# A two-block transformer in split precision: where weights' low parts are made, where modulation columns are computed, and when two groups of transposes are issued

## The chip, the cores and the metric

The kernel runs on one core of a Trainium2 chip. The metric is the time of one execution on the device in microseconds, lower is better; the median of several runs is given, and beside it the time of one execution that was taken with a profile. Engines are named as the profile names them: PE is TensorE (PEld its weight loads), DVE is VectorE, ACT is ScalarE, POOL is GpSimd, SP is SyncE, whose queue issues most DMAs.

## The reference, cut to what matters

The sequence has 512 tokens and the model 1024 channels, in fp32. The first block has two layers that are modulated by a condition vector `c`, and a second block follows.

```python
for layer in range(2):
    mod = silu(c) @ ada_w[layer] + ada_b[layer]
    sh_m, sc_m, g_m, sh_f, sc_f, g_f = split(mod, 6)
    h = modulate(rms_norm(x, pre_mix_g[layer]), sh_m, sc_m)
    y = gmlp_mixer(h, ...) if layer == 0 else fox_mixer(h, ..., k, v, dcum)
    x = x + g_m * rms_norm(y, post_mix_g[layer])
    h = modulate(rms_norm(x, pre_ffn_g[layer]), sh_f, sc_f)
    x = x + g_f * rms_norm(swiglu(h, ...), post_ffn_g[layer])
    if layer == 0:
        k, v, dcum = shared_kv(x, silu(c) @ kv_ada_w + kv_ada_b, ...)
...
def gmlp_mixer(h, ...):
    u, v = split(gelu(h @ w_in + b_in), 2)
    ...
    return y @ w_out
def shared_kv(x, mod_kv, ...):
    kvf = modulate(rms_norm(x), shift, scale) @ kv_w     # keys, values, forget gates
    k = rms_norm(k, k_norm_g)                            # per head of 64
    ...
```

The second block projects its normed input to an mLSTM's and a sparse attention's parts: `m_q`, `m_k`, `m_if` (gates) and `ix_q`, `ix_k`, `ix_w` (an indexer, whose scores choose 128 keys for each query) are among them. It ends with an output projection, a gated addition and a norm.

## The kernel before, in words

Every fp32 product is made of three TensorE products (`mm3`, L415 to L418): each operand is split into a high part, rounded to the type that TensorE takes, and a low part, the remainder. A weight tile of 128 x 1024 is loaded on SP's queue into one of four `raw` buffers (L271). ACT copies the high part (`whi`, L279). The low part (`wlo`, L282) is a subtraction on DVE, or, for every `share`-th tile, on POOL; a share of 0 keeps all on DVE. There are four buffers each for `whi` and `wlo`.

Products come in two forms. `gemm_a` takes one weight tile for one tile of 128 output features and 512 tokens: 24 matmuls, called a chunk. `gemm_b` (L459) holds four PSUM accumulators, one for each 128 tokens, for a group of 512 output features, and goes through the weight tiles of the group, two rows of 128 channels in each, again 24 matmuls a chunk. With `tail` the last chunks of the last group go token tile by token tile; with `head` the whole first group does, and its share is `hshare`. PSUM has two sets of four tiles: accumulators (`acc`) and transposes (`tp`).

The modulation is not a matmul. Its 96 columns are computed one by one on DVE: SP loads 128 x 1024 of `ada_w` into a `raw` buffer (L298), and one DVE operation multiplies by `silu(c)` and sums (L302, in place). `fill(n)` makes n such calls on average, each loading one column's weights and computing the column that was loaded by the call before, so 97 calls make 96 columns. `need(c0)` forces calls until a column is there. Calls are spread over the GEMMs by `nfill`: 1.25 for each chunk of `w_v` (L793), 0.75 for each of `w_ao` (L856), and 2 for each chunk of the gate-up of layer 0 from its 10th on (L432, L602). Ahead of `w_ao`, L854 needs the columns of the next norm. After a gate-up, L603 makes what calls are left.

The order of the stages around the change: the gMLP's `w_v` (groups 1 to 3, four chunks each), `w_u` (`gemm_a`), `w_ao` (two groups of eight chunks; its evacuation `post`, L550 to L573, starts with a DVE product at L558 and feeds `halves`, which transposes into the next GEMM's operands), the gate-up and the down product of the first feed-forward part, and then the shared keys and values. The keys (`w_k`, two groups, L1094) are normed for each head by `headnorm` (L873), and at the last token tile `kdone` (L1074) makes for each group 16 PE transposes (L959, in `pair_t`), four ACT copies (L1081), four DVE operations (L1082) and 16 DMA issues on POOL to a scratch (`spread`, L938). `forget` (L1098) follows, then the operands `hx` of the queries (eight times a load on SP, an ACT operation, and two DVE operations, L1123 to L1128), then the values (`w_vv`, two groups of four chunks, L1129, share 1, so all low parts on POOL) and the queries (`w_q`, L1133).

In the second block the indexer's projection `w_ix` ends with the gates. From them the kernel makes columns: four PE transposes at L1248 of ACT's `iwt` (L1244), eight at L1268, two DVE copies, and an ACT exponential; the DVE chain between ends at L1257 to L1259. Then comes `w_aqk` (L1291), whose evacuation `ev_a` runs after each chunk, and then the masks.

A scheduler at build time fixes the order in each engine's queue, from a model of durations and from what each instruction depends on, taking what comes first in the program among what is ready; a few stages, which the change does not touch, are written out by hand. Temporary tiles of 128 x 512 (`T`) rotate through nine buffers, which `kdone`, `forget` and the `hx` loop share.

Of the kernel before, what the change touches and what calls it, by code (L numbers as in the profile page):

```python
# [16 lines left out]
AF = mybir.ActivationFunctionType  # L17
# [3 lines left out]
P = 128  # L21
T_ = 512
NT = 4
# [21 lines left out]
KS = 2  # L45
KH = 3
VS = 1
# [144 lines left out]
def body(tc, nc, a):  # L192
    V, S_, G, PE = nc.vector, nc.scalar, nc.gpsimd, nc.tensor

    with ExitStack() as es:
# [31 lines left out]
        def acc():  # L227
            return tile_of(ps, "acc")
# [230 lines left out]
        def gemm_b(h, w, groups, kt, evac, head=False, tail=0, nfill=0, share=0, raws=(), hshare=1):  # L459
# [5 lines left out]
            for gi in groups:  # L465
# [8 lines left out]
                for c in range(nch - tm):  # L474
                    wh, wl = wsplit(w[gi, c], share=share, raw=raws.pop(0) if raws else None)
                    fill(nfill)
                    for t in range(NT):
                        part(t, c, wh, wl)
                ws = []
# [95 lines left out]
        def halves(h, g, sh, spill=None):  # L575

            xn = {}

            def done(t, n):
                xn[t] = n  # L580
                if t % 2:
                    to_T((t - 1, t), xn, g, sh, *h, spill=spill)
            return done
# [32 lines left out]
        with tc.tile_pool(name="l0", bufs=20) as p0:  # L616
# [176 lines left out]
            gemm_b(h, a["w_v"], range(1, 4), KD, ev_v, nfill=1.25, share=3, raws=early_w)  # L793
# [46 lines left out]
            def ev_u1(i, pt):  # L840
# [5 lines left out]
                else:  # L846
# [7 lines left out]
            gf, sf = gain(32, "pfg0"), need(24)  # L854
            hf = hpair()
            gemm_b((yh, yl), a["w_ao"], range(2), 16, post(gb, xs[0], xs[1], L, halves(hf, gf, sf)), tail=4,  # L856
                   nfill=0.75, share=2)
# [6 lines left out]
        def nxt0():  # L864
            hk.extend(hpair())
            return halves(hk, gain(104, "kvg"), need(96), xT)
# [5 lines left out]
        def headnorm(out, alloc, done=None):  # L872
# [3 lines left out]
            def evac(g, t, pt):  # L876
# [8 lines left out]
                if t == NT - 1:  # L885
                    rsq(ss[:, 32:64], ss[:, 0:32], 1.0 / 64)
                    for q in range(NT):
                        r = ss[:, 32 + q * 8:40 + q * 8]
                        V.tensor_mul(b3(raw[q], 8), b3(raw[q], 8), r.unsqueeze(2).broadcast_to((P, 8, 64)))
                        out[q, g] = raw[q]  # L890
                        if done:
                            done(g, q, raw[q])
# [172 lines left out]
        with tc.tile_pool(name="x", bufs=1) as px:  # L1065
# [8 lines left out]
            def kdone(g, t, ap):  # L1074

                if t < NT - 1:
                    return
# [17 lines left out]
            gemm_b(hk, a["w_k"], range(2), KD, headnorm(kt_, ka, kdone), head=True, share=KS, hshare=KH)  # L1095
# [3 lines left out]
            def forget():  # L1099
# [7 lines left out]
                pt = acc()  # L1107
# [21 lines left out]
            gemm_b(hk, a["w_vv"], range(2), KD, lambda g, t, pt: vsplit(g, t, pt, va, vdone), share=VS)  # L1129
# [77 lines left out]
        def nxt1():  # L1207
            h.extend(hpair())
            return halves(h, vc("nin", 0, 8), None)
# [3 lines left out]
        with tc.tile_pool(name="z", bufs=NZ) as pz:  # L1213
# [32 lines left out]
            pt = tp()  # L1246
            for t in range(NT):
                PE.transpose(pt[:, t * 12:(t + 1) * 12], iwt[0:12, t * P:(t + 1) * P], ident[0:12, 0:12])  # L1248
            V.tensor_copy(iw[:], pt[:, 0:48].rearrange("p (t h) -> p t h", t=NT)[:, :, 4:12])
# [14 lines left out]
            pt = tp()  # L1264
            for q, src in enumerate((la, lt)):
                for t in range(NT):
                    o_ = (q * NT + t) * 4
                    PE.transpose(pt[:, o_:o_ + 4], src[0:4, t * P:(t + 1) * P], ident[0:4, 0:4])  # L1268
            V.tensor_copy(am[:], pt[:, 0:32].rearrange("p (q t h) -> p q t h", q=2, t=NT))
            S_.activation(am[:, 1, :, :], am[:, 1, :, :], AF.Exp, scale=-1.0)  # L1270
# [8 lines left out]
            def ev_a(i, pt):  # L1279
# [9 lines left out]
                else:  # L1289
                    spread(d, (1, 2, 4, 5), hi, lo)  # L1290
            gemm_a(h, a["w_aqk"], 2, ev_a, share=2)  # L1291
# [343 lines left out]
```

## Time and profile before

| what | value |
|---|---|
| median of 3 runs | 1892.88 us (1891.61 to 1895.67) |
| the profiled execution's own time | 1890.45 us |
| its span, from first to last instruction | 1888.6 us |
| mean granted TensorE clock | 0.989 of full speed |
| PE busy | 1823.4 us, 97% of the span |
| DMA | 305.75 MB, 162 GB/s over the span |

Times in the rows are microseconds from the start of the span. The order of the stages in it: `w_ao` begins at 229.8, the gate-up at 328, the down product at 577, the keys at 699, the values at 756, the queries at 818, and `w_aqk` at 1430. In a timeline a row is one instruction or a run of alike ones (x4): start, time in us, engine, line, operation, output <- input and shapes, and in brackets how long the engine had waited and for what. Engine names with a q (SPq) are the DMA issues of that engine's queue.

### The profile page before, as it was taken

To read this page: it belongs to the slowest core of one execution; us is meant where nothing else is said; L and a number is where in the kernel's file an instruction comes from. 1 tells how busy PE (TensorE), PEld (TensorE's weight loads), DVE (VectorE), ACT (ScalarE), POOL (GpSimd) and SP (SyncE) were. 2 spreads that over 40 slices of the span, in tenths; PEclk is the share of its full clock that TensorE was granted. 3 is DMA by queue.
4 is the path that set the end of the run, shared out by engine and by line. 5 is a ranking of instruction groups with operands and counts; after the bars stand their busy time and mean duration, and the time that the engine had idled before them with its cause. 6 is when DMAs were issued, how large, how long until landed. Compare 5 with 4: busy or idle time off the path is not lost. (4 is left out here: it accounts for less than half of the span.)

```text
span 1888.6 us, 23901 instructions
## 1 busy us (share of the span) xinstructions
PE 1823.4 (97%) x8688; PEld 1506.0 (80%) x8688; DVE 1116.9 (59%) x2144; ACT 789.8 (42%) x1395; POOL 409.1 (22%) x316
## 2 busy tenths in 40 slices
PE   7999989999999999699999999999999999999997
PEld 5788868988778877587878888888887878888886
DVE  7879843677772255529886433332268978746524
ACT  5333324422232245448875422222256356455334
POOL 2110121222120024653332111110012563031022
PEclk9999999999999999899999999999999999999999
DMA  9684662477773436744533322332435543322532
GB/s 337 229 285 143 229 210 91 161 265 263 250 261 107 143 127 209 246 145 158 182 118 113 111 100 90 101 102 100 145 117 184 195 162 125 112 95 93 180 111 80
DMA packets 101967, 305.75 MB, mean 162 GB/s; under 512 B 12277, under 2 KB 13085, under 8 KB 101850
## 3 DMA queue, kind: packets, MB, share of 16 engines
q1 hardware_dynamic: 93402, 276.96, 43.9%
q0 software_dynamic: 8448, 27.27, 4.2%
q8 instruction: 69, 1.13, 0.2%
q14 instruction: 48, 0.39, 0.1%
HBM read 269.50 MB, written 37.30 MB: 162 GB/s over the span
## 5 line engine op out<-in xcount | busy, mean ns | idle before, releaser
L279 ACT ACTIVATE whi<-raw 128x1024 fp32r<-128x1024 f32 x281 | 296.7, 1058 | 661.4 <-PE acc L418 302.1
L282 POOL TENSOR_TENSOR wlo<-raw,whi 128x1024 fp32r<-128x1024 f32 x112 | 273.3, 2443 | 893.3 <-ACT whi L279 825.9
L282 DVE TENSOR_TENSOR wlo<-raw,whi 128x1024 fp32r<-128x1024 f32 x169 | 214.7, 1273 | 301.8 <-ACT whi L279 278.8
L418 PE MATMUL acc<-h,wlo 128*128 128x512 f32 x896 | 350.0, 391 | 3.0 <-DVE wlo L282 3.0
L416 PE MATMUL acc<-h,whi 128*128 128x512 f32 x896 | 350.8, 392 | 0.8 <-DVE s L903 0.5
L417 PE MATMUL acc<-h,whi 128*128 128x512 f32 x896 | 349.6, 390 | 0.0
L417 PE MATMUL acc<-wlo,h 128*128 128x512 f32 x608 | 240.8, 397 | 16.0 <-POOL wlo L282 15.7
L416 PE MATMUL acc<-whi,h 128*128 128x512 f32 x608 | 241.7, 399 | 6.6 <-DVE h L408 6.6
L418 PE MATMUL acc<-whi,h 128*128 128x512 f32 x608 | 240.4, 397 | 0.0
L418 PEld LDWEIGHTS acc<-h,wlo 128*128 128x128 f32 x896 | 168.6, 188 | 40.2 <-DVE wlo L282 5.1
L416 PEld LDWEIGHTS acc<-h,whi 128*128 128x128 f32 x896 | 168.7, 188 | 36.9 <-issue 1.7
L302 DVE SCALAR_TENSOR_TENSOR raw<-raw,cact 128x1024 f32<-128x1024 f32 x96 | 151.6, 1589 | 76.6 <-DMA raw<-in_ada 75.2
L417 PEld LDWEIGHTS acc<-h,whi 128*128 128x128 f32 x896 | 168.5, 188 | 34.4
L417 PE MATMUL acc<-wlo,s 128*128 128x512 f32 (+1 forms) x488 | 190.7, 391 | 0.0
L416 PE MATMUL acc<-whi,s 128*128 128x512 f32 (+1 forms) x488 | 190.4, 390 | 0.2 <-DVE t L1321 0.2
L418 PE MATMUL acc<-whi,s 128*128 128x512 f32 (+1 forms) x488 | 190.2, 390 | 0.0
L417 PEld LDWEIGHTS acc<-wlo,h 128*128 128x128 f32 x608 | 116.0, 191 | 40.6 <-POOL wlo L282 16.9
L416 PEld LDWEIGHTS acc<-whi,h 128*128 128x128 f32 x608 | 115.3, 190 | 30.7 <-DVE h L408 7.8
L418 PEld LDWEIGHTS acc<-whi,h 128*128 128x128 f32 x608 | 115.7, 190 | 26.3 <-DVE h L409 2.6
L416 PEld LDWEIGHTS acc<-whi,s 128*128 128x128 f32 x488 | 91.7, 188 | 19.5 <-DVE t L1321 0.6
L417 PEld LDWEIGHTS acc<-wlo,s 128*128 128x128 f32 x488 | 91.7, 188 | 18.8
L418 PEld LDWEIGHTS acc<-whi,s 128*128 128x128 f32 x488 | 91.7, 188 | 18.7
(371 smaller groups left out, 2710.0 us busy)
## 6 DMA issues: line engine op xcount, KB each, us to landing
raw<-in_ada SPq DMA_DIRECT2D x96, 512.0 KB, 4.1
raw<-in_w_gu SPq DMA_DIRECT2D x88, 512.0 KB, 3.5
raw<-in_w_dn SPq DMA_DIRECT2D x44, 512.0 KB, 3.2
scr<-t POOLq DMA_DIRECT2D x56, 256.0 KB, 5.5
raw<-in_w_o SPq DMA_DIRECT2D x20, 512.0 KB, 3.4
row<-scr SPq DMA_DIRECT2D x36, 256.0 KB, 3.0
d<-in_ada SPq DMA_DIRECT2D x16, 512.0 KB, 7.2
raw<-in_w_v SPq DMA_DIRECT2D x16, 512.0 KB, 5.0
```

The costliest lines, as they stand in the source:

```text
L279: S_.activation(hi[:, 0:n], raw[:, 0:n], AF.Copy)
L282: e.tensor_sub(lo[:, 0:n], raw[:, 0:n], hi[:, 0:n].bitcast(F32))
L302: V.scalar_tensor_tensor(raw, raw, 1.0, cact[0], ALU.mult, ALU.mult, accum_out=modc[:, col:col + 1])
L416: PE.matmul(out, lh, rh, start=start, stop=False)
L417: PE.matmul(out, lh, rl, start=False, stop=False)
L418: PE.matmul(out, ll, rh, start=False, stop=stop)
```

## The change

Five edits. The shares of `w_v`, `w_ao`, `w_k` (beyond its head group) and `w_vv` go, so that their 4, 8, 2 and 8 low parts on POOL are made on DVE. In `gemm_b`, `fill` is left out at a group's first and last chunk, and the rates are 2 for `w_v` and 1.5 for `w_ao`. The modulation that `halves` needs is asked for when the first normed tile arrives, not ahead of the GEMM, so nothing is forced ahead of `w_ao`. `kdone` of the first key group runs after the first chunk of the second group, and that of the second after the first chunk of `w_vv` (so also after `forget` and the `hx` loop); `forget`'s PSUM tile comes from the transposes' set. The indexer's and gates' columns are made after the first `w_aqk` chunk's evacuation.

```diff
-KS = 2
-VS = 1
...
-        def gemm_b(h, w, groups, kt, evac, head=False, tail=0, nfill=0, share=0, raws=(), hshare=1):
+        def gemm_b(h, w, groups, kt, evac, head=False, tail=0, nfill=0, share=0, raws=(), hshare=1, then={}):
...
                 for c in range(nch - tm):
                     wh, wl = wsplit(w[gi, c], share=share, raw=raws.pop(0) if raws else None)
-                    fill(nfill)
+
+                    if 0 < c < nch - 1:
+                        fill(nfill)
                     for t in range(NT):
                         part(t, c, wh, wl)
+                    if c == 0 and gi in then:
+                        then[gi]()
...
-        def halves(h, g, sh, spill=None):
+        def halves(h, mod, spill=None):
 
-            xn = {}
+            xn, gs = {}, []
 
             def done(t, n):
+                if not gs:
+                    gs.extend(mod())
                 xn[t] = n
                 if t % 2:
-                    to_T((t - 1, t), xn, g, sh, *h, spill=spill)
+                    to_T((t - 1, t), xn, *gs, *h, spill=spill)
             return done
...
-            gemm_b(h, a["w_v"], range(1, 4), KD, ev_v, nfill=1.25, share=3, raws=early_w)
+            gemm_b(h, a["w_v"], range(1, 4), KD, ev_v, nfill=2, raws=early_w)
...
-            gf, sf = gain(32, "pfg0"), need(24)
             hf = hpair()
-            gemm_b((yh, yl), a["w_ao"], range(2), 16, post(gb, xs[0], xs[1], L, halves(hf, gf, sf)), tail=4,
-                   nfill=0.75, share=2)
+            gemm_b((yh, yl), a["w_ao"], range(2), 16,
+                   post(gb, xs[0], xs[1], L, halves(hf, lambda: (gain(32, "pfg0"), need(24)))), tail=4,
+                   nfill=1.5)
...
-            def kdone(g, t, ap):
-
-                if t < NT - 1:
-                    return
+            def kdone(g):
+
                 for pr in range(4 * g, 4 * g + 4):
...
-            gemm_b(hk, a["w_k"], range(2), KD, headnorm(kt_, ka, kdone), head=True, share=KS, hshare=KH)
+            gemm_b(hk, a["w_k"], range(2), KD, headnorm(kt_, ka), head=True, hshare=KH, then={1: lambda: kdone(0)})
...
-                pt = acc()
+                pt = tp()
...
-            gemm_b(hk, a["w_vv"], range(2), KD, lambda g, t, pt: vsplit(g, t, pt, va, vdone), share=VS)
+            gemm_b(hk, a["w_vv"], range(2), KD, lambda g, t, pt: vsplit(g, t, pt, va, vdone),
+                   then={0: lambda: kdone(1)})
...
+            def columns():
+
+                pt = tp()
+                for t in range(NT):
+                    PE.transpose(pt[:, t * 12:(t + 1) * 12], iwt[0:12, t * P:(t + 1) * P], ident[0:12, 0:12])
+                V.tensor_copy(iw[:], pt[:, 0:48].rearrange("p (t h) -> p t h", t=NT)[:, :, 4:12])
+                pt = tp()
+                for q, src in enumerate((la, lt)):
+                    for t in range(NT):
+                        o_ = (q * NT + t) * 4
+                        PE.transpose(pt[:, o_:o_ + 4], src[0:4, t * P:(t + 1) * P], ident[0:4, 0:4])
+                V.tensor_copy(am[:], pt[:, 0:32].rearrange("p (q t h) -> p q t h", q=2, t=NT))
+                S_.activation(am[:, 1, :, :], am[:, 1, :, :], AF.Exp, scale=-1.0)
...
                     spread(d, (1, 2, 4, 5), hi, lo)
+                if i == 0:
+                    columns()
             gemm_a(h, a["w_aqk"], 2, ev_a, share=2)
```

The same instructions as those of `columns` are taken out where they stood (L1246 to L1249 and L1264 to L1270). The other two users of `halves` get the same arguments as before, within a `lambda`.

## Rows read from the trace of the kernel before

**Rows 1.** The page's first part: busy time of each engine, share, instructions.
```profile
PE 1823.4 (97%) x8688; PEld 1506.0 (80%) x8688; DVE 1116.9 (59%) x2144; ACT 789.8 (42%) x1395; POOL 409.1 (22%) x316
```

**Rows 2.** Waits of PE: line waited for, total us, times, longest.
```profile
PE acc L417 <- POOL wlo L282: 15.7, 2, 14.6
PE acc L416 <- DVE t L558: 7.0, 1, 7.0
...
PE tp L1248 <- ACT t L1244: 1.9, 1, 1.9
PE tp L959 <- issue: 1.8, 1, 1.8
```

**Rows 3.** Windows: length, PE, PEld, DVE, ACT, POOL busy, clock, DMA, GB/s.
```profile
229.82:273.34 43.52, 43.52 (x195) 35.87 (x192) 18.27 (x22) 12.32 (x18) 10.43 (x4) 1.00 0.63 215
280.66:284.11 3.45, 3.45 (x9) 2.76 (x10) 1.74 (x3) 0.00 (x0) 0.00 (x0) 0.53 0.95 309
...
773.01:779.02 6.01, 6.01 (x14) 4.77 (x15) 2.44 (x1) 0.81 (x1) 6.01 (x3) 0.51 0.92 305
1430.64:1434.28 3.64, 3.64 (x10) 2.84 (x9) 1.31 (x2) 3.58 (x4) 0.00 (x0) 0.53 0.07 14
...
699.00:751.59 52.59, 48.78 (x225) 38.66 (x224) 34.37 (x65) 26.79 (x50) 23.73 (x29) 1.00 0.66 216
```

**Rows 4.** Timeline of PE, start of the values.
```profile
757.47 0.94 PE L416 MATMUL acc<-whi,h 128*128 128x512 f32 x3
773.01 0.80 PE L417 MATMUL acc<-wlo,h 128*128 128x512 f32 x1 [14.59 <-POOL wlo L282]
```

**Rows 5.** Timeline of POOL, start of the values.
```profile
758.73 0.60 POOL L938 DMA_DIRECT2D scr<-t  x1 [10.06 <-ACT t L1081]
...
769.99 0.60 POOL L938 DMA_DIRECT2D scr<-t  x1 [0.15 <-issue]
770.60 9.32 POOL L282 TENSOR_TENSOR wlo<-raw,whi 128x1024 fp32r<-128x1024 f32 x4
```

**Rows 6.** Timeline of ACT, high parts ahead of the values.
```profile
740.96 1.06 ACT L279 ACTIVATE whi<-raw 128x1024 fp32r<-128x1024 f32 x1 [4.35 <-issue]
...
756.68 1.04 ACT L279 ACTIVATE whi<-raw 128x1024 fp32r<-128x1024 f32 x1
```

**Rows 7.** Timeline of DVE, around the values.
```profile
748.40 0.69 DVE L883 TENSOR_REDUCE hn<-gb 128x8 f32<-128x512 f32 x1 [11.21 <-ACT gb L881]
...
776.58 4.88 DVE L1127 CAST hm<-t 128x512 fp32r<-128x512 f32 x1 [8.86 <-ACT t L1126]
...
790.60 0.42 DVE L1127 CAST hm<-t 128x512 fp32r<-128x512 f32 x1
```

**Rows 8.** One line's instructions: ns min/median/max, first and last start, shapes.
```profile
L282 DVE TENSOR_TENSOR wlo<-raw,whi x169: 1185/1225/3409, 9.4 to 1857.4; 128x1024 fp32r<-128x1024 f32 x169
L282 POOL TENSOR_TENSOR wlo<-raw,whi x112: 2340/2397/3427, 10.8 to 1834.8; 128x1024 fp32r<-128x1024 f32 x112
...
L302 DVE SCALAR_TENSOR_TENSOR raw<-raw,cact x96: 1206/1225/3421, 75.7 to 552.7; 128x1024 f32<-128x1024 f32 x96
...
L395 POOL DMA_DIRECT2D scr<-t x8: 707/727/732, 695.2 to 720.4; - x8
```

**Rows 9.** Timeline of DVE, the gates' chain.
```profile
1437.75 0.68 DVE L1257 TENSOR_TENSOR t<-t,t 4x512 f32<-4x512 f32 x1
```

**Rows 10.** Timelines of SP and DVE, `w_ao`'s change of groups.
```profile
270.10 0.33 SPq L298 DMA_DIRECT2D raw<-in_ada  x1
...
275.94 2.92 DVE L302 SCALAR_TENSOR_TENSOR raw<-raw,cact 128x1024 f32<-128x1024 f32 x1 [5.87 <-DMA raw<-in_ada]
...
279.93 2.47 DVE L558 TENSOR_TENSOR t<-acc,gb 128x512 f32<-128x512 f32 x4
```

**Rows 11.** Timeline of SP, the gate-up's weight loads towards its end.
```profile
486.07 0.37 SPq L271 DMA_DIRECT2D raw<-in_w_gu  x1
...
498.49 0.37 SPq L271 DMA_DIRECT2D raw<-in_w_gu  x1
...
548.91 5.36 SPq L271 DMA_DIRECT2D raw<-in_w_gu  x3
```

**Rows 12.** Windows of PE alone, the gate-up: length, PE busy, clock, DMA, GB/s.
```profile
485.00:510.00 25.00, 24.45 (x108) 1.00 0.72 248
510.00:535.00 25.00, 23.08 (x99) 1.00 0.76 250
535.00:552.00 17.00, 16.32 (x70) 1.00 0.77 258
```

More of the change, by code (lines that the diff above doesn't have):

```diff
@@ L865, in nxt0 @@
             hk.extend(hpair())
-            return halves(hk, gain(104, "kvg"), need(96), xT)
+            return halves(hk, lambda: (gain(104, "kvg"), need(96)), xT)
         ffn(0, hf, xs[1], xs[2], lambda: gb_row(40, "qfg0"), nxt0)
@@ L871, in body, with headnorm @@
         cmask = const("cmask", [P, P], "mask")
-        def headnorm(out, alloc, done=None):
+        def headnorm(out, alloc):
             st = {}
@@ L890, in evac @@
                         out[q, g] = raw[q]
-                        if done:
-                            done(g, q, raw[q])
             return evac
@@ L1208, in nxt1 @@
             h.extend(hpair())
-            return halves(h, vc("nin", 0, 8), None)
+            return halves(h, lambda: (vc("nin", 0, 8), None))
         ffn(1, hf, xs[3], xs[4], lambda: gb_row(88, "qfg1"), nxt1)
@@ L1245, in body @@
             iw = pc.tile([P, NT, 8], F32, name="iw")
[L1246 to L1249, printed above, removed]
+            def columns():
[10 more added lines that the diff above has]
+                S_.activation(am[:, 1, :, :], am[:, 1, :, :], AF.Exp, scale=-1.0)
             lf, lt, la, lm, on = T(), T(), T(), T(), T()
@@ L1263, in body @@
             am = pc.tile([P, 2, NT, 4], F32, name="am")
[L1264 to L1270, printed above, removed]
             av = {}
```

## The prediction

> **What bounds the kernel now.** I read the engines' shares first [rows 1]: PE is busy 97% of the span, so whatever is to be had lies in the 3% in which PE waits, or in stretches where it runs below full clock; DVE at 59% and POOL at 22% matter only where PE waits for them. Next PE's waits, by what released them [rows 2]. The largest is 14.6 us for one low part on POOL (L282); then 7.0 for DVE's L558, 1.9 for ACT's L1244 and 1.8 at L959, which waits for nothing shown. All four lie where the diff works. Then the windows [rows 3]. With PE always fed, 192 weight loads' worth of matmuls take 43.52 us, 0.2267 each, and a chunk of 24 takes 5.44. Behind each of three large waits stands a stretch at granted clock 0.51 to 0.53, which is the 1.2 GHz level of the two, and PE had idled just before: 14 matmuls in 6.01 us where 3.17 were due (2.84 lost), 9 in 3.45 (1.41 lost), 10 in 3.64 (1.37 lost). So a wait that goes takes its cold tail with it.
>
> The least obvious wait needs the queues. PE stops at 758.42 after one product and goes on 14.59 us later [rows 4]. The low part that it wants sits on POOL behind 16 DMA issues of the keys' scratch (L938), 0.60 each, which waited 10.06 for ACT's L1081 and run from 758.73 to 770.60; four low parts follow in 9.32 [rows 5]. The high parts were ready between 740.96 and 757.72 [rows 6], and DVE, which could have made the low parts, idled 11.21 before 748.40 [rows 7]. That is a queue in the wrong order, not a lack of engine time.
>
> **The change, part by part.**
>
> *Low parts to DVE.* 22 of them (8 of values, 2 of keys, 4 of `w_v`, 8 of `w_ao`) leave POOL at 2.397 us and come to DVE at 1.225 [rows 8]: 27 us more on an engine with some 770 idle, spread over stages where DVE has room (34.37 busy of 52.59 in the keys, 18.27 of 43.52 ahead of `w_ao`) [rows 3]. I cost that at nothing; PE's 97% covers it. For the values, the queue of [rows 5] no longer stands ahead, the high parts are there, and the wait goes with its tail: 14.59 + 2.84 = **17.4**. Bounds: 0, if another queue takes the place (rival 3), and 17.4.
>
> *Keys' transposes one chunk later.* 16 PE transposes, 4 ACT copies, 4 DVE operations and 16 POOL issues per group move behind the first chunk of the next group. On PE, 24 matmuls now cover the norm that the transposes follow, so L959's wait goes: **1.8** (0 to 1.8). The SP queue is not touched by them; but the loads of `hx` (SP, into the buffers that the second group's parts also use) now stand ahead of the second group's issues on POOL. The 16 issues of group 1 then run beside the value chunks, with no low part behind them on POOL. `forget`'s accumulator comes from the other pair of PSUM tiles: nothing, since that stage shows no wait in [rows 2].
>
> *Indexer's and gates' columns.* 12 transposes, two DVE copies and one ACT operation go behind the first `w_aqk` chunk. The wait of 1.90 and the tail of 1.37 make 3.3 at most. The chain that feeds them ends on DVE at 1437.75 + 0.68 [rows 9], about as late as that chunk's end, and the masks' use of them is no earlier; I take **2.0** (0 to 3.3).
>
> *`w_ao`: no modulation columns at the handover.* DVE's L558 is late there, behind a column product (L302) which waited 5.87 for a load that SP issued at 270.10 and then ran 2.92 instead of its usual 1.225 [rows 8, 10]. In the new order the last call of group 0 is at chunk 6, the first of group 1 at chunk 1, so neither stands in the queue at the switch. 7.03 + 1.41 = 8.4 at most. But group 1's chunks 1 to 3 carry 1, 2 and 1 calls where they carried 0.75 each, and its low parts now share DVE with the columns and L558; I leave 2.0 for that and take **6.4** (-2 to 8.4).
>
> *The gate-up that pays.* Calls are moved, not removed: 97 are needed. `w_v` makes 12 instead of 15, `w_ao` 13 instead of 9, and the ten that were forced ahead of `w_ao` go. So 25 instead of 34 are made when the first gate-up begins, and that makes two for each chunk from its 10th to its 43rd, 68 in all. Before, 63 were left and the last product started at 552.7 [rows 8], two to three chunks before the end; after, 72 are left, all chunks carry two, and four calls (three loads) fall between gate-up and `w_dn0`. With two columns per chunk the loads of two chunks take 498.49 - 486.07 = 12.42 us [rows 11], while PE wants 10.88, or 0.77 more per chunk. PE lived on weights loaded ahead till about 500; from there it loses (0.55, 1.92, 0.68 us in three stretches [rows 12]), and after 548.91 loads come free of columns [rows 11]. Three more paced chunks cost 3 x 0.77 = 2.3. The three loads ahead of `w_dn0`'s first cost 3.7 at DVE's rate (3 x 1.225) or 6.2 at the stream's (3 x 2.07, six loads per 12.42); I take 3.7, since no chunk's loads stand between them. **-6.0** (0, if weights loaded ahead hide it, to -9.9 with the stream's rate and a tail of 1.41). `w_dn0` carries no columns, so nothing is given back further on.
>
> Sum: 17.4 + 1.8 + 2.0 + 6.4 - 6.0 = 21.6. The profiled execution took 1890.45, 2.43 under the median of the runs. 1890.45 - 21.6 = 1868.85; on the median **1871.3**.
>
> **Rivals.**
>
> 1. *Gate-up pays nothing and the handover is free*: the stream has slack at its end, as its weights loaded ahead showed till 500. 6.0 + 2.0 + 1.3 more: 1871.3 - 9.3 = 1862. Against it: the losses of [rows 12]. Chance 0.18.
> 2. *The handover wait stays*: group 1's low parts on DVE take the place of the column product ahead of L558. 1871.3 + 6.4 = 1877.7, with gate-up's worst 1881.6, with a handover worse by 2 1883.6. For it: four L558 already take 2.47 in one run [rows 10]. Chance 0.17.
> 3. *The change doesn't do what it says*: the value chunks' wait moves to another releaser, and 1871.3 + 17.4 = 1888.7 results, with the keys' wait back 1890.5: no change. Against it: high parts early and DVE idle [rows 6, 7]. Chance 0.06.
> 4. *Slower: the low part stuck in DVE's queue.* DVE runs in order, and the casts of `hx` (L1127) wait for loads into buffers that the keys' 16 POOL issues hold; before, they ran from 776.58 to 790.60 after 8.86 of waiting [rows 7]. If a value low part stands behind them, PE waits until they are through. Point of decision: chunks 2 to 4 can be made ahead, so the fifth low part is wanted at 757.5 + 4 x 5.44 = 779.2. A wait W there gives 1871.3 + W + 2.84 for the tail, which is 0.2% slower when W is over 22.5, that is with the casts through at about 802; at 805 it gives some 1900. I expect them through at about 764, because `hx` now waits for the first group's issues only: half of the keys' 52.59 us after 699 is 725, a chunk of 5.44 and 16 issues of 0.60 make 741, and 8.86 of waiting and 14.4 of casts, as before, 764. It would take 38 us more over 16 issues: 2.4 more each. Against it: POOL's issues beside DVE casts on another line took 0.73 against 0.60 [rows 5, 8], 2 us over 16. Chance 0.05.
>
> The Trainium skill, page "SBUF — State Buffer", section "SBUF: two separate sides" (the "DVE blocks DMA" box), speaks for rival 4: a DMA issued from POOL has its descriptors written by GpSimd, which is locked out of the shared port while DVE runs a 2-port operation. A later section of that page gives some 620 ns alone and 3100 overlapped; by that, an estimate of 16 x 2.5 = 40 us would be past the point. By the trace's 0.73 it agrees in direction and not in size, and so the chance stays at 0.05.
>
> **How the numbers follow.** The forecast has 0.54, rivals 1 to 4 have 0.18, 0.17, 0.06, 0.05. A measurement of this kernel can tell 0.2%, 3.8 us, from no change. Forecast and rivals 1 and 2 are all faster by more: 0.89. Rival 3 is within: 0.06. Rival 4 is slower: 0.05. The range reaches from rival 1 with a little more, 1861, to rival 2's worst, 1884, and leaves out rivals 3 and 4.
>
> **What would show it.** Right: no POOL low part among PE's waits at L417; L959 and L1248 without waits over 0.5; a value stage of some 44 us at granted clock 1.00; at `w_ao`'s switch L416 waiting under 2 us; the last column product after gate-up's end, near 575, with a new wait of 3 to 6 us at the start of `w_dn0`. Wrong: a DVE wait of over 10 us in the value stage, the L558 wait still at 7, or PE idle in a stage that the diff leaves alone, the masks for one, where DVE may get the same work earlier or later.

## The result, and the profile after

The changed kernel takes 1874.77 us (median of 4 runs, 1873.22 to 1877.14) beside 1894.28 for the kernel before (four runs; the 1892.88 that the forecast starts from is the median of the first three). The ratio is 0.9898 with a 95% interval of 0.988 to 0.9915. The forecast was 1871.3 in a range of 1861 to 1884. The runs further down were made in four series, in which the kernel before took 1890.17 to 1891.78; the ratio in brackets behind a run's time is to the kernel before in its own series, with the interval. The profiled execution took 1873.39 us, 17.06 less than the one that the sum was made against, where the sum said 21.6.

First the page's own line of the engines, against [rows 1], and three of the costliest groups, which the edits touch.

```profile
PE 1822.3 (97%) x8688; PEld 1504.1 (80%) x8688; DVE 1126.0 (60%) x2166; ACT 789.9 (42%) x1395; POOL 357.9 (19%) x294
...
L280 DVE TENSOR_TENSOR wlo<-raw,whi 128x1024 fp32r<-128x1024 f32 x191 | 238.3, 1251 | 303.8 <-ACT whi L277 285.0
...
L280 POOL TENSOR_TENSOR wlo<-raw,whi 128x1024 fp32r<-128x1024 f32 x90 | 221.7, 2465 | 673.0 <-ACT whi L277 593.7
...
L300 DVE SCALAR_TENSOR_TENSOR raw<-raw,cact 128x1024 f32<-128x1024 f32 x96 | 146.4, 1536 | 76.7 <-DMA raw<-in_ada 73.9
```

The 22 low parts are where the change puts them (POOL 112 to 90, DVE 169 to 191), and DVE is busy only 9.1 us more, not 27. PE's busy time is the same to 1.1 us: what was gained is, in the main, time in which PE stood still.

All traces hold 8688 matmuls, so a stage can be taken from the start of the same matmul, by number, in each (the first from the start of the span, the others from nos. 233, 985, 1384, 2554, 3099, 3546, 6552, 6694, 6989). Lengths in us, of the profiled execution of each kernel; the names are those of the runs below.

| kernel | first stage | `w_v`, `w_u` | `w_ao` | gate-up | down | keys and values | queries to `w_ix` | `w_aqk` | masks |
|---|---|---|---|---|---|---|---|---|---|
| before | 74.07 | 155.75 | 98.18 | 249.06 | 122.14 | 119.31 | 608.70 | 32.87 | 67.70 |
| after | 72.32 | 155.68 | 89.45 | 253.91 | 122.96 | 106.98 | 608.81 | 32.76 | 67.64 |
| e1 | 72.38 | 155.68 | 89.30 | 253.30 | 122.95 | 122.17 | 608.83 | 34.35 | 67.68 |
| e2 | 74.26 | 155.71 | 97.67 | 247.59 | 122.15 | 114.62 | 609.90 | 33.28 | 67.69 |
| e3 | 74.43 | 155.68 | 89.33 | 252.01 | 122.97 | 107.69 | 609.77 | 32.73 | 67.69 |
| e4 | 72.92 | 155.68 | 89.30 | 259.72 | 136.87 | 107.43 | 609.13 | 32.81 | 67.69 |
| e5 | 73.38 | 155.68 | 89.32 | 254.16 | 122.94 | 100.74 | 610.17 | 35.47 | 67.68 |
| e5b | 73.25 | 155.68 | 89.31 | 252.18 | 122.94 | 99.44 | 616.80 | 34.05 | 67.66 |
| e6 | 74.00 | 155.68 | 89.30 | 252.16 | 122.96 | 106.15 | 608.35 | 36.35 | 67.01 |
| e8 | 74.19 | 155.68 | 92.18 | 252.33 | 122.71 | 107.51 | 610.12 | 33.15 | 67.68 |
| e9 | 72.47 | 155.68 | 95.66 | 248.19 | 122.16 | 106.73 | 611.46 | 34.37 | 67.66 |
| e10 | 73.82 | 155.68 | 91.06 | 249.01 | 122.16 | 101.05 | 608.55 | 34.30 | 67.68 |
| e12 | 73.42 | 155.68 | 95.18 | 249.07 | 122.16 | 107.88 | 607.69 | 34.23 | 67.68 |
| e13 | 73.25 | 155.70 | 90.45 | 243.35 | 122.16 | 100.39 | 608.32 | 32.73 | 67.69 |

Each row is one execution. `w_v` with `w_u` agrees to 0.1 us in all of them, and so do the masks but for e6. Other stages move from one execution to the next with the same code in them: the first by 2.1 us, the queries to `w_ix` by 3.8 (without e5b), `w_aqk` by 2.7 (32.73 to 35.47, with the same waits of PE), the gate-up by 2.2 (252.01 to 254.16 in the runs that leave it as in the changed kernel), and keys and values by 1.7 (106.15 to 107.88). A smaller difference in one of these stages tells nothing by itself. So 1.75 of the 17.06 us come from the first stage, which has no edit. The rest of the change, after less before: `w_ao` -8.73, gate-up +4.85, down +0.82, keys and values -12.33, `w_aqk` -0.11.

PE's waits in the changed kernel (line waited for, total us, times, longest) show the places.

```profile
PE acc L414 <- DVE h L406: 5.2, 4, 2.2
PE acc L416 <- DVE wlo L280: 4.0, 5, 1.0
PE acc L414 <- ACT k L889: 3.5, 1, 3.5
...
PE acc L414 <- DVE t L603: 2.6, 5, 1.3
PE tp L1259 <- DVE t L1269: 2.2, 1, 2.2
...
PE tp L1253 <- ACT t L1246: 1.2, 1, 1.2
```

Of the four waits of [rows 2] three are gone: POOL's low part, the DVE product at `w_ao`'s switch, and the transposes' 1.8. The fourth, 1.9 for ACT's L1244, has become 1.2 (L1246) and a second one of 2.2 (L1269). New is ACT's L889, 3.5 us at the first accumulator of the values.

That one, by its queues: PE, ACT, POOL and SP of the changed kernel, around the end of the keys.

```profile
752.36 0.80 PE L414 MATMUL acc<-whi,h 128*128 128x512 f32 x1 [3.54 <-ACT k L889]
```

```profile
744.01 0.82 ACT L1127 ACTIVATE t<-t,modc,gcol 128x512 f32<-128x512 f32 x1 [8.61 <-DMA t<-scr]
746.34 0.82 ACT L1127 ACTIVATE t<-t,modc,gcol 128x512 f32<-128x512 f32 x1 [1.51 <-DMA t<-scr]
...
750.53 0.81 ACT L1127 ACTIVATE t<-t,modc,gcol 128x512 f32<-128x512 f32 x1 [2.43 <-DMA t<-scr]
751.25 0.58 ACT L886 ACTIVATE gb<-acc 128x512 f32<-128x512 f32 x1
751.73 0.58 ACT L889 ACTIVATE k<-acc 128x512 f32<-128x512 f32 x1
```

```profile
740.61 0.61 POOL L941 DMA_DIRECT2D scr<-t  x1 [0.29 <-DMA scr<-t]
```

```profile
739.60 9.90 SPq L1126 DMA_DIRECT2D t<-scr  x4
```

These rows are one chain through four queues. POOL issues the first key group's scratch until 741. By the program, the issues hold temporary tiles, and the loads of the queries' operands need such tiles; four of the eight loads go out on SP between 739.6 and 749.5. ACT has the operation on the fourth operand (L1127 at 750.53, after 2.43 us of waiting for its load) ahead of the evacuation of the keys' accumulators (L886, L889). PE wants one of these accumulators at 748.82. Windows of the same kernel (length; then busy time and instructions of PE, PEld, DVE, ACT, POOL; clock; DMA; GB/s) show what it costs.

```profile
748.82:752.36 3.54, 0.00 (x0) 0.00 (x0) 1.59 (x3) 1.83 (x4) 0.00 (x0) 0.85 0.88 277
752.36:757.50 5.14, 5.14 (x12) 4.08 (x13) 4.79 (x10) 5.14 (x10) 0.00 (x0) 0.50 0.85 297
```

PE stands for 3.54 us, and then 12 matmuls take 5.14 at a granted clock of 0.50, the 1.2 GHz level, where 2.72 were due: 3.54 + 2.42 = 6.0 us. The DMA engines are busy 0.88 of the time during the wait, so these rows do not tell whether the loads come late for the tiles that are held or for the traffic of the issues beside them.

### The profile page after: what moved, and what is told of

The parts are those of the page before. It is cut to its first block, busy times and chain, and to the rows that moved or that the text cites. A ratio compares the mean times of both kernels' runs of the same rounds, so it can differ in the third digit from the quotient of the medians.

```text
span 1871.5 us, 23902 instructions
## 1 busy us (share of the span) xinstructions
PE 1822.3 (97%) x8688; PEld 1504.1 (80%) x8688; DVE 1126.0 (60%) x2166; ACT 789.9 (42%) x1395; POOL 357.9 (19%) x294
## 5 line engine op out<-in xcount | busy, mean ns | idle before, releaser
L280 DVE TENSOR_TENSOR wlo<-raw,whi 128x1024 fp32r<-128x1024 f32 x191 | 238.3, 1251 | 303.8 <-ACT whi L277 285.0
L280 POOL TENSOR_TENSOR wlo<-raw,whi 128x1024 fp32r<-128x1024 f32 x90 | 221.7, 2465 | 673.0 <-ACT whi L277 593.7
L300 DVE SCALAR_TENSOR_TENSOR raw<-raw,cact 128x1024 f32<-128x1024 f32 x96 | 146.4, 1536 | 76.7 <-DMA raw<-in_ada 73.9
L572 POOL DMA_DIRECT2D scr<-s x24 | 13.3, 556 | 541.5 <-DVE s L571 540.4
L414 PEld LDWEIGHTS acc<-whi,s 128*128 128x128 f32 x488 | 91.7, 188 | 20.4 <-DVE t L1328 1.0
```

The source lines that it names most:

```text
L280: e.tensor_sub(lo[:, 0:n], raw[:, 0:n], hi[:, 0:n].bitcast(F32))
L300: V.scalar_tensor_tensor(raw, raw, 1.0, cact[0], ALU.mult, ALU.mult, accum_out=modc[:, col:col + 1])
L414: PE.matmul(out, lh, rh, start=start, stop=False)
L572: nc.gpsimd.dma_start(xdst[rows, h * 512:(h + 1) * 512], xr[h])
```

## The experiments

**e1 and e2: the two parts of the value edit by themselves.** e1 is the changed kernel with the values' low parts on POOL again; e2 is the kernel before with the shares of values and keys taken away and nothing else.

```diff
-                   then={0: lambda: kdone(1)})
+                   share=1, then={0: lambda: kdone(1)})
```

> The changed kernel, with the values' eight low parts put back on POOL (share 1 in w_vv). Theory: the old 14.6 us wait came from the order of POOL's queue, 16 scratch issues ahead of the low parts, and not from POOL's speed; with the keys' transposes moved, POOL is idle from 741 to 765, so eight low parts of 2.4 us keep up with chunks of 5.44 and the time is 0 to 5 us above the changed kernel's 1874, with no wait for POOL's low part over 3 us. Rival: it is the faster engine that brought the gain; the value stage loses 10 us or more again, 1884 to 1891.

```diff
-gemm_b(hk, a["w_k"], ..., head=True, share=KS, hshare=KH)
+gemm_b(hk, a["w_k"], ..., head=True, hshare=KH)
...
-gemm_b(hk, a["w_vv"], ..., share=VS)
+gemm_b(hk, a["w_vv"], ...)
```

> The kernel before, with only the low parts of the values and of the keys' second group on DVE, the keys' transposes left where they were. Theory: taking the low parts out of POOL's queue is enough by itself; the 14.6 us wait goes, some 3 us of it come back as a wait behind the operands of the queries, and the profiled time is 10 to 17 us under the 1890.5 of before. Rival: the order of the transposes decides, and the value stage waits 10 us or more for another engine that stands behind the 16 issues (ACT's or DVE's operations on the queries' operands): within 4 us of 1890.5.

e1 took 1891.14 us (ratio to before 0.9996, 0.9983 to 1.0009), e2 1885.26 (0.9973, 0.9955 to 0.999). Both theories fall. e1's time is the one that its rival gave, for another reason; e2 has the wait that its rival gave, and 4.4 us less than before in the profiled execution. Keys and values take 119.31 before, 122.17 in e1, with the transposes moved, 114.62 in e2, with the low parts moved, and 106.98 with both. The parts do not add: the first loses 2.9, the second gains 4.7, and both gain 12.3 (the keys' two low parts are on DVE in both runs). POOL's queue in e1:

```profile
739.72 2.40 POOL L280 TENSOR_TENSOR wlo<-raw,whi 128x1024 fp32r<-128x1024 f32 x1
760.54 0.63 POOL L941 DMA_DIRECT2D scr<-t  x1 [18.41 <-ACT t L1082]
...
769.76 3.87 POOL L941 DMA_DIRECT2D scr<-t  x6 [0.63 <-DMA scr<-t]
773.65 9.34 POOL L280 TENSOR_TENSOR wlo<-raw,whi 128x1024 fp32r<-128x1024 f32 x4
```

POOL was free from 742 to 760, as the theory said, and could do nothing with it: the build's order puts the second group's issues behind the first low part and ahead of the next four, and the first issue waits 18.41 us for ACT. PE waits 9.7 for the low part. It is the order, not POOL's speed (2.4 us each): moving the transposes in the program did not move their issues behind the low parts. In e2 the low parts no longer wait, and PE's stop comes later, at the values' change of groups (PE, then ACT, then DVE):

```profile
787.62 0.77 PE L416 MATMUL acc<-whi,h 128*128 128x512 f32 x1 [11.99 <-DVE v L903]
```

```profile
774.14 0.82 ACT L1126 ACTIVATE t<-t,modc,gcol 128x512 f32<-128x512 f32 x1 [6.37 <-DMA t<-scr]
...
781.96 0.36 ACT L901 ACTIVATE v<-acc 128x256 fp32r<-128x256 f32 x1
```

```profile
774.99 0.43 DVE L1127 CAST hm<-t 128x512 fp32r<-128x512 f32 x1 [4.55 <-ACT t L1126]
...
787.20 0.28 DVE L903 TENSOR_TENSOR v<-acc,v 128x128 fp32r<-128x128 f32 x1
```

ACT (L1126) and DVE (L1127) have the operands of the queries ahead of the values' evacuation (L901, L903) in their queues, and those wait for loads that come after the 16 issues. So the issues reach PE by two ways, over POOL's low parts and over the operands' loads. The change closes the first with the low parts and shortens the second by its order; neither edit does both.

**e5 and e5b: the operands' loads out of the issues' way.** e5 makes the queries' operands ahead of the first group's transposes; e5b puts both groups' transposes into the values.

```diff
-gemm_b(hk, a["w_k"], ..., then={1: lambda: kdone(0)})
+gemm_b(hk, a["w_k"], ..., then={1: lambda: (operands(), kdone(0))})
```

Here `operands` is the `hx` loop, taken from behind `forget`.

> The changed kernel, with the loop that makes the queries' operands ahead of the first group's transposes, after the first chunk of the keys' second group. Theory: the 3.5 us wait for ACT's L889 at the start of the values, new in the changed kernel, is an order in ACT's queue: an operation on the queries' operands that waits for a load stands ahead of the evacuation of the keys' accumulators, and the load waits for temporary buffers that the 16 scratch issues hold. With the operands first the wait goes with its tail at half clock, 6 to 7 us in all, 1866 to 1869. Rival: the loads of the operands then make ACT wait inside the keys' stage, and PE waits there or at the values' start by 3 us or more: 1872 to 1880.

```diff
-gemm_b(hk, a["w_k"], ..., then={1: lambda: kdone(0)})
+gemm_b(hk, a["w_k"], ...)
...
-                   then={0: lambda: kdone(1)})
+                   then={0: lambda: kdone(0), 1: lambda: kdone(1)})
```

> The changed kernel, with both groups' transposes in the values' stage (the first group's after the first chunk of the values' first group, the second's after that of the second), so that no scratch issue stands between the keys and the loads of the queries' operands. Theory as for the run before: ACT's wait at the values' start goes, 6 to 7 us, 1866 to 1869. Rival: 32 issues beside the values hold temporary buffers that the values or the queries need, or DVE and ACT meet them at the values' change of groups, and a wait of 5 us or more comes there: 1872 to 1885.

e5 took 1869.19 us (0.9882, 0.9855 to 0.991). Keys and values fall to 100.74, 6.24 under the changed kernel, as the 3.54 and its tail of 2.42 say; no wait in the stage is over 1.1 us. That shows the chain above, from the operands' place to PE's wait; it does not part the held tiles from the traffic. The profiled execution (1872.77) is the longest of e5's four: the queries and `w_aqk` took 4.1 us more in it, of the size that these stages move by themselves. e5b took 1875.62 (0.991, 0.9877 to 0.9942): keys and values are shorter still, 99.44, and the queries' stage gives 8.0 back (616.80). PE waits there for a low part on POOL (the 4.9):

```profile
PE acc L415 <- POOL wlo L280: 6.0, 2, 4.9
```

This part of the queries' weights again stands behind issues in POOL's queue. The rival's time holds, but the wait is not in one of the places that it named.

**e3, e8, e9, e12: what made the wait at `w_ao`'s switch.** e3 has columns at every chunk again, at rates that leave the 25 calls as they are; e8 puts every second low part of `w_ao` back on POOL; e9 makes 34 calls by rates of 1.25 and 1.6; e12 forces 13 columns ahead of `w_ao`.

```diff
-                    if 0 < c < nch - 1:
-                        fill(nfill)
+                    fill(nfill)
...
-gemm_b(h, a["w_v"], ..., nfill=2, ...)
+gemm_b(h, a["w_v"], ..., nfill=1, ...)
...
-                   nfill=1.5)
+                   nfill=1.1)
```

> The changed kernel, with modulation columns again at every chunk of w_v and w_ao, the first and last of a group too, at rates (1 and 1.1) that make the same 25 calls before the gate-up. Theory: it is the column product in DVE's queue where the accumulators change hands that made PE wait; the wait for DVE's first product of the evacuation is back with 4 to 8 us and a tail at half clock of 1.4, and the time is 1878 to 1884. Rival: the columns forced ahead of w_ao and POOL's share were the cause; the wait stays under 2 us and the time at 1872 to 1876.

```diff
-                   nfill=1.5)
+                   nfill=1.5, share=2)
```

> The changed kernel, with every second low part of w_ao on POOL again. Theory: as columns at the switch did no harm with the low parts on DVE, it was POOL's low parts that made the column's load and product late (four raw buffers, one held 2.4 us and more, and a DVE product of 2.9 beside POOL); the wait for L558's counterpart at the switch is back with 3 us or more and the time is 1876 to 1883. Rival: the ten columns forced ahead of w_ao, which are gone here too, were the cause; the wait stays under 1 us and the time within 2 us of the changed kernel beside it.

e9 is e3's edit with `nfill=1.25` and `nfill=1.6` in its last two lines.

> The changed kernel, with columns at every chunk at rates of 1.25 in w_v and 1.6 in w_ao, so that 34 calls are made before the gate-up as in the kernel before, but none forced ahead of w_ao. Theory: the 5.4 us that the changed kernel loses at the gate-up's end come from the nine calls put off into it; with 34 made, PE loses there the 3 us of the kernel before and the time is 1867 to 1870. Rival: w_ao can't carry them, a wait of 4 us or more comes at its switch or its end, and the time is 1872 or more.

```diff
+            mod0 = (gain(32, "pfg0"), need(24))
             hf = hpair()
...
-... lambda: (gain(32, "pfg0"), need(24)))
+... lambda: mod0)
```

> The changed kernel, with the modulation of the next norm asked for ahead of w_ao again, so that 13 columns are forced there (12 are made by then and 25 are needed) and 13 more run in w_ao: 38 calls ahead of the gate-up. Theory: forced columns run on into w_ao through the four raw buffers and the product before the switch comes late: a wait for L561 of 3 us or more at the switch, with what the gate-up gives back (its last waits go) within 3 us of the changed kernel beside it. Rival: the burst is over long before the switch; no wait there, and the gate-up's 5 us come back: 1867 to 1870.

e3 took 1874.42 us, the changed kernel's time, and PE waits nowhere at the switch: the theory falls, and with it a part of the reason that the prediction gave. e8 took 1881.77 (0.9947, 0.9927 to 0.9967; a wait of 2.6), e9 1876.12 (0.9915, 0.9887 to 0.9942; 3.3) and e12 1873.28 (0.9908, 0.9886 to 0.9931; 4.0). So the theories of e8 and e12 hold (e8 with a little less than its 3 us), and in e9 the rival. DVE at the switch in the changed kernel, e3, e8 and e12, each with the last column product and the first products of the evacuation; the first group's last matmul ends at 271.80, 273.92, 273.68 and 272.93.

```profile
268.60 1.23 DVE L300 SCALAR_TENSOR_TENSOR raw<-raw,cact 128x1024 f32<-128x1024 f32 x1 [3.40 <-DMA raw<-in_ada]
```

```profile
269.63 1.23 DVE L300 SCALAR_TENSOR_TENSOR raw<-raw,cact 128x1024 f32<-128x1024 f32 x1 [1.84 <-DMA raw<-in_ada]
271.93 1.28 DVE L560 TENSOR_TENSOR t<-acc,gb 128x512 f32<-128x512 f32 x2
```

```profile
273.22 1.23 DVE L300 SCALAR_TENSOR_TENSOR raw<-raw,cact 128x1024 f32<-128x1024 f32 x1 [4.24 <-DMA raw<-in_ada]
275.50 2.48 DVE L561 TENSOR_TENSOR t<-acc,gb 128x512 f32<-128x512 f32 x4
```

```profile
273.89 1.22 DVE L300 SCALAR_TENSOR_TENSOR raw<-raw,cact 128x1024 f32<-128x1024 f32 x1 [2.33 <-DMA raw<-in_ada]
276.18 2.47 DVE L561 TENSOR_TENSOR t<-acc,gb 128x512 f32<-128x512 f32 x4
```

A column product does stand ahead of the evacuation in each, in e3 too. What differs is when it ends against the group: 3.1 us earlier in e3, 0.8 later in e8, 2.2 later in e12; in the changed kernel 2.0 earlier (269.83 against 271.80), and before it was 5.2 later (278.86 by [rows 10], against 273.64). So keeping columns from the switch is not what took the wait away.

Counted in the traces, 25 products have run when the evacuation starts in the changed kernel, in e3 and in e8, 34 before, 33 in e9 and 38 in e12. (The program has four of the changed kernel's 25 behind the switch; the queue has all of them ahead of it.) Two things make the last product late. One is POOL's low parts, with the same 25 products: 2.73 us of stage length in e8. The other is the number of products: with no low part of `w_ao` on POOL, 25 give no wait, 30 give 1.4 us (e10) and 0.8 (e13), 33 give 3.3 and 38 give 4.0, for which e12 pays 5.73 us of stage length. The two prices make 8.46, of the 8.73 that the stage lost; that they add is not shown, and e12 has four products more than the kernel before.

**e4, e10, e13: what the gate-up pays for columns.** e4 lowers the gate-up's rate from 2 to 1.5 calls for each chunk and gives the rest to the middle chunks of the down product.

```diff
-gemm_a(h, a[f"w_gu{l}"], 2 * KF, evac, group=4, nfill=2, ...)
-while len(done) < len(ADA):
-    fill()
+gemm_a(h, a[f"w_gu{l}"], 2 * KF, evac, group=4, nfill=1.5, ...)
...
-gemm_b((hh, hl), a[f"w_dn{l}"], ..., share=DS[l])
+gemm_b((hh, hl), a[f"w_dn{l}"], ..., share=DS[l], nfill=1.5)
+while len(done) < len(ADA):
+    fill()
```

> The changed kernel with the gate-up making 1.5 calls for each chunk instead of 2, and the first down product taking 1.5 for each of its middle chunks instead of none (forced calls, if any are left, after it). Theory: the gate-up's end pays because two columns and a weight tile want three loads in 5.44 us and the stream gives one in 2.07; at 2.5 loads (5.2 us) it pays nothing, in the gate-up or in the down product. The waits at the end of the gate-up go (8 to 9 us with the three that the kernel before had), and the time is 1864 to 1867. Rival: the loads are only moved, and the down product waits for them: 1871 to 1876.

e4 took 1901.27 us (1.0052, 1.003 to 1.0073), slower than both. Its profiled execution, 1893.82, is the fastest of ten, so what the others lose beyond it is in no trace. In it the gate-up makes fewer calls and takes 259.72, 5.8 more, and the down product takes 13.9 more. The window from 440 to 570, and DVE's column products from 440 to 600 (total busy, mean ns of one; idle before them and for what), first of the changed kernel:

```profile
440.00:570.00 130.00, 123.15 (x529) 97.95 (x528) 98.69 (x127) 32.08 (x42) 23.99 (x10) 1.00 0.78 256
```

And its column products:

```profile
L300 DVE SCALAR_TENSOR_TENSOR raw<-raw,cact 128x1024 f32<-128x1024 f32 x43 | 72.4, 1700 | 24.2 <-DMA raw<-in_ada 24.2
```

The same window of e4:

```profile
440.00:570.00 130.00, 119.30 (x504) 92.86 (x503) 83.49 (x96) 30.12 (x40) 31.50 (x10) 1.00 0.61 210
```

Its column products, and its low parts on DVE, again from 440 to 600:

```profile
L300 DVE SCALAR_TENSOR_TENSOR raw<-raw,cact 128x1024 f32<-128x1024 f32 x38 | 46.5, 1225 | 51.7 <-DMA raw<-in_ada 51.6
L280 DVE TENSOR_TENSOR wlo<-raw,whi 128x1024 fp32r<-128x1024 f32 x14 | 36.7, 2625 | 0.0
```

With the lower rate DMA is busy 0.61 of the time instead of 0.78, and PE is busy less as well. What PE waits for in e4 from 440 to 606, and DVE ahead of the longest of these waits:

```profile
PE acc L416 <- DVE wlo L280: 10.3, 10, 1.2
PE acc L414 <- DVE t L603: 10.2, 2, 8.4
```

```profile
592.21 1.23 DVE L300 SCALAR_TENSOR_TENSOR raw<-raw,cact 128x1024 f32<-128x1024 f32 x1 [3.11 <-DMA raw<-in_ada]
...
593.37 0.68 DVE L603 TENSOR_TENSOR t<-t,acc 128x512 f32<-128x512 f32 x1
```

The two longer waits are in the down product: L603, which makes its operand, stands in DVE's queue behind column products that wait for their loads. The ten short ones are in the gate-up, and each is for a low part on DVE. Nine of these ten low parts take 3.4 us; the usual time is 1.22. POOL is at work on its own low part beside each of them. In the changed kernel it is a column product that meets POOL (POOL, then DVE):

```profile
547.45 2.41 POOL L280 TENSOR_TENSOR wlo<-raw,whi 128x1024 fp32r<-128x1024 f32 x1 [10.19 <-ACT whi L277]
```

```profile
547.53 3.40 DVE L300 SCALAR_TENSOR_TENSOR raw<-raw,cact 128x1024 f32<-128x1024 f32 x1 [0.20 <-DMA raw<-in_ada]
```

Of the changed kernel's 43 products from 440 to 570, the ten that start while POOL makes a low part take 3.28 us on average, and the other 33 take 1.22; that is the mean of 1700 ns above. So a DVE operation of this size that starts beside a low part on POOL takes 2 us longer, and the order decides which one it is: in e4 it is the low part that PE wants next. e4's gate-up got slower for that reason (these waits are 10.3 us, beside 6.6 in the changed kernel's gate-up; 2.1 of the 5.8 stay open), and e4 cannot say whether the stream of weights paces the gate-up, which is the price that the prediction used. The slowed operations led to the last run. e10 is e5 with 30 calls ahead of the gate-up (every chunk of `w_v` at 1.25, the middle chunks of `w_ao` at 1.7); e13 is e10 with one constant changed.

> Operands first as in the run of that name, and columns at every chunk of w_v at 1.25 (15 calls) and at the middle chunks of w_ao at 1.7 (15), so 30 calls ahead of the gate-up and none at w_ao's switch. Theory: the gate-up's loss goes with its number of calls, 5.4 us for nine of them, so five fewer give 2 to 4 us back, and the values 6: 1864 to 1868. Rival: the calls in w_v and w_ao make waits there, as at 1.6 for every chunk, and the time is that of the operands alone, 1868 to 1872.

```diff
-GU = (2, 3)
+GU = (0, 3)
```

> The kernel with the operands first and 30 calls ahead of the gate-up (1867.0), with the first gate-up's low parts all on DVE too; every second stood on POOL. Theory: the gate-up's loss comes from POOL's low parts, which hold one of four raw buffers 2.4 us, and beside which column products take up to 3.4 us instead of 1.2; with them on DVE (DVE is busy 98.6 of 130 us there, and 10 more of 1.2 fit) the waits at the gate-up's end go and the time is 1861 to 1865. Rival: the column products wait in DVE's queue for their own loads (20 us between 440 and 570), whoever makes the low parts; with more of these behind them PE waits as long or longer, 1866 to 1872.

e10 took 1867.03 us (0.9873, 0.9851 to 0.9896), as its theory said: the gate-up is at 249.01, 4.9 shorter for five calls, `w_ao` 1.6 longer. e13 took 1859.99 (0.9852, 0.982 to 0.9883), the fastest of all and a little faster than its theory said; no execution of it is as long as the shortest of e10. The gate-up's waits are gone: its stage is 243.35, 5.7 under the kernel before. The same two views of e10:

```profile
440.00:570.00 130.00, 126.30 (x551) 102.32 (x550) 98.61 (x124) 36.89 (x48) 24.04 (x10) 1.00 0.77 258
```

Its column products:

```profile
L300 DVE SCALAR_TENSOR_TENSOR raw<-raw,cact 128x1024 f32<-128x1024 f32 x39 | 66.5, 1721 | 20.1 <-DMA raw<-in_ada 19.5
```

And of e13:

```profile
440.00:570.00 130.00, 130.00 (x576) 107.52 (x575) 88.71 (x131) 37.57 (x48) 0.00 (x0) 1.00 0.75 255
```

Its column products:

```profile
L300 DVE SCALAR_TENSOR_TENSOR raw<-raw,cact 128x1024 f32<-128x1024 f32 x37 | 45.3, 1225 | 24.1 <-DMA raw<-in_ada 23.6
```

PE is busy 130.00 of 130, at nearly the same 255 GB/s (e10 has 258). So two columns and a weight tile for each chunk do not make the stream the limit. DVE has twelve low parts more and is busy 9.9 us less, mainly because no product is slowed. Column products wait for their own loads no less than in e10 (23.6 beside 19.5), so it wasn't these waits, and the rival falls. Whether POOL's low parts cost PE time here by the slowed products or by a longer hold on a raw buffer was not tried apart.

**e6: the columns one chunk later still.**

```diff
-                if i == 0:
+                if i == 1:
                     columns()
```

> The changed kernel, with the indexer's and gates' columns after the second w_aqk chunk instead of the first. Theory: PE's 2.2 us wait at the gates' transposes is there because their chain (ACT's two table loads, DVE's scans) ends 2 us after the first chunk; after the second it is over, and the wait goes: 2 to 3.5 us under the changed kernel's profile of 1873.4 in that stage, with the wait of 1.2 for ACT ahead of the first chunk gone or not, as the build's order has it. Rival: the masks, DVE's longest stretch, start that much later and PE waits at their end instead; the stage up to the second attention is not shorter by over 0.5 us.

e6 took 1878.05 us (0.9934, 0.9909 to 0.9958), and the stage takes 36.35, longer by 3.6, of which up to 2.7 may be the movement of this stage with the same code. The theory falls: the wait for L1269 has not gone but grown. The rival's number holds (nothing gained), but not its reason, since the masks take no longer (67.01). PE in e6 and, second, in the changed kernel:

```profile
1415.04 0.41 PE L1253 MATMUL tp<-ident,t 12*128 12x12 f32 x4
1419.88 0.59 PE L1259 MATMUL tp<-ident,t 4*128 4x4 f32 x4 [3.54 <-DVE t L1269]
```

```profile
1412.41 0.41 PE L1253 MATMUL tp<-ident,t 12*128 12x12 f32 x4 [1.23 <-ACT t L1246]
...
1421.39 0.41 PE L1259 MATMUL tp<-ident,t 4*128 4x4 f32 x4 [2.21 <-DVE t L1269]
```

The transposes are not where the program has them. In the changed kernel the first four still come ahead of the first `w_aqk` chunk, and in e6 L1259 still comes right behind the first chunk, its 3.54 us of waiting ahead of the second. The build's order goes by what its model of durations takes for ready; that the model has the gates' chain earlier than the chip fits these rows, and no run shows it.

## Why the prediction was right, point by point

*Values, 17.4.* The direction and the wait that went are right; the size was off. With the keys' 1.8 the sum had 19.2 for the two stages, and 12.3 were measured. The step that failed is "the wait goes with its tail: 14.59 + 2.84", with nothing put in its place. Rival 4 had the mechanism that took 6.0 of it, loads of the operands behind the issues and an in-order engine behind the loads, but looked for it on DVE and at the fifth chunk; it came on ACT, ahead of the evacuation that frees the first accumulator, a place that the working did not ask about. It was far too small to turn the sign. The cover that was named, that `hx` waits only for the first group's issues, held nearly: the issues ended at 741, as worked out, the casts were not through at 764 but at 759.06 (758.70 + 0.36), and yet ACT was late for its other work.

*The Trainium skill's rule* (page "SBUF — State Buffer", section "SBUF: two separate sides") beside rival 4: in the changed kernel the keys' issues on POOL took 0.61 us each, also beside a DVE cast, so no run here shows one held up by the estimate of 2.5 (POOL, then DVE):

```profile
734.56 2.42 POOL L941 DMA_DIRECT2D scr<-t  x4 [0.79 <-ACT t L1127]
```

```profile
734.34 0.43 DVE L1128 CAST hm<-t 128x512 fp32r<-128x512 f32 x1 [3.08 <-ACT t L1127]
```

What the runs do show of POOL and DVE beside each other is DVE's side: 3.28 us for a product that starts beside a low part on POOL, 1.22 for one that doesn't.

*Keys, 1.8.* L959's wait is gone, and the same 16 transposes now run without one behind a chunk; from matmul no. 3099 to no. 3280 the changed kernel gains 1.75 us (42.87 to 41.12). That the move did it is not shown: in e2, with the transposes left in their place and the low parts moved, the wait is gone too, and the same matmuls take 41.03.

*Columns, 2.0.* Measured 0.1, in a stage that moves by 2.7. The step "go behind the first `w_aqk` chunk" failed: the program's place does not bind the queue's. The bound of 0 held.

*`w_ao`, 6.4 of at most 8.4.* Measured 8.7, all of it. The sum's residue was not needed, but the reason is only half right: e3 shows columns at the switch without a wait. By e8, e9, e10 and e12 the last product is early because fewer products have run by then and no low part of `w_ao` is on POOL.

*Gate-up, -6.0.* Measured 4.85 + 0.82 = 5.7, with the calls moved as counted, and e9, e10 and e12 get about 5 us back with 30 to 38 calls made earlier. The size was right for a wrong reason, and that is luck. The terms of 2.07 per load took the stream for the limit, and e13 shows that it isn't. The wait of 3 to 6 us that was forecast for the start of `w_dn0` is 0.3, and the last product ends ahead of the gate-up's end (571.36), not near 575:

```profile
568.42 1.23 DVE L300 SCALAR_TENSOR_TENSOR raw<-raw,cact 128x1024 f32<-128x1024 f32 x1 [0.54 <-DMA raw<-in_ada]
```

The loss lies within the gate-up instead, in ten waits of 0.2 to 1.3 us from 497 on, 6.6 in all, where the kernel before has six with 3.2.

*The rest.* The sum of the terms is 4.5 us larger than what the profiles show; the first stage, with no edit in it, hides 1.75 more, so the terms missed by 6.3: values and keys by 6.9 and columns by 1.9, of which `w_ao` made good 2.3. So the sum came out nearer than its largest term. Of the rivals, 1 happened in its half about the handover; 2 did not, and neither did 3, since the new wait is a quarter of the old.

## What to carry to other kernels

Before a wait is written off, ask of every engine that works in order, and not only of the one that waited, what else stands in its queue behind the same late transfer; here one set of 16 issues reached PE over POOL, over DVE and over ACT, and each edit closed one way. Where a build step sets the queues' order from a model of durations, a move in the source is a wish: look at the order in the trace. And where work on one engine slows another, count the time of what runs beside it: taking work from the slow engine made the fast one less busy.

## What the runs showed that was not expected

Moving the gate-up's low parts from POOL to DVE took 9.9 us off DVE's busy time in the window (98.61 to 88.71), since a column product fell from 1721 to 1225 ns (39 in 66.5 us, then 37 in 45.3). Fewer columns per chunk made the gate-up longer (259.72 beside 253.91) with DMA less busy (0.61 beside 0.78), since DVE's low parts, and no longer column products, then ran beside POOL's and took 3.4 us instead of 1.22. And two edits of the values' stage that cost 2.9 us and gain 4.7 alone gain 12.3 together.
